# Residual updates in widely spaced pieces beside the feed-forward part, and an S5 input product that opens with two blocks

## The chip, the cores and the metric

The kernel runs on one core of a Trainium2 chip. The metric is the device time of one launch in microseconds (us), as a median of runs. TensorE (PE) does the matrix products, VectorE (DVE), ScalarE (ACT) and GpSimd (POOL) the elementwise work, and SyncE (SP) issues most of the DMAs. TensorE's clock is granted at one of two levels, 1.2 or 2.4 GHz; the profile gives the granted clock of a stretch as a share of the higher one.

## What is computed

One inference step of a two-layer encoder trunk, for 1024 prompt tokens and 32 sample tokens that share all weights (model width 1024, feed-forward width 4096, all in float32):

```
for layer in range(2):
    h = rmsnorm(x, g0);  mix = retention + forgetting attention  (layer 0)   or   S5 state space + GLU  (layer 1)
    x = x + rmsnorm(mix, g1)
    h = rmsnorm(x, g2);  x = x + rmsnorm(cross_attn(h, memory), g3)
    h = rmsnorm(x, g4);  x = x + rmsnorm(square(relu(h @ w_up)) @ w_down, g5)
# S5: u = h @ w_in_c; states x_t = a * x_(t-1) + B u_t; y = C x + D u; then a gate
```

Every `x = x + rmsnorm(...)` is a residual update. The order that matters here: cross-attention and its update in layer 0, feed-forward in layer 0 and its update, the S5 input product of layer 1, the S5 scan, the second layer's memory products, the gate product, and then cross-attention and feed-forward of layer 1.

## The kernel before, in words

Activations lie transposed: 128 rows of the width on the partitions, tokens along the free dimension. The 1056 tokens are cut into three groups of 384, 384 and 288. A float32 product is made of three matmuls of rounded parts (`mm3`, L72: high x high, high x low, low x high), so each weight block is split on arrival into `wh` (ScalarE, L139) and `wl` (VectorE, L140), and each activation tile into `xh` (ScalarE, L201) and `xl` (VectorE, L202). A block of 128 output rows for one group is 8 x 3 = 24 matmuls.

TensorE's instructions run in exactly the order in which the program writes them; the other engines' order is chosen by a scheduler that goes by readiness and by a priority, which is the place in the program minus an offset (300 for update pieces and for evacuations, and 600 for the first weights of the feed-forward part). So the place in the program of a piece of VectorE work only gives its priority, while the place of a matmul is binding.

Small dependent steps are placed among the matmuls by a hand-made order, `po`. It keeps a clock `po.now`, which every matmul advances by its columns / 2400 (in us). `po.later(dt, fn)` puts a step into a queue, due `dt` later; `po.tick()`, called after each three matmuls of a block, runs what is due; `po.until(cond)` runs the next steps at once, due or not, until `cond` holds. `get(out, g, key)` is such a demand for a group's input tiles `X` or its scale row or column `r`.

A residual update (`update`, L247) of one group runs through these steps. `post_scale` sums the squares of the product's output over the width (three matmuls with `ones_c` into a bank `c`, from the accumulator `acc`), and takes the root on GpSimd. `add` broadcasts the result to rows (matmuls into a bank `b`). Then come eight pieces `part(0)` to `part(7)`, one for each 128 rows: load the residual (SP), scale (DVE, L273), add (DVE or POOL, L274), split into `xh` and `xl` for the next product, store the new residual (issued by ACT), and square it and add it to `acc2` (ACT and POOL, L244 and L245). `pre_scale` then sums `acc2` over the width (matmuls into a bank `a`) and takes the root (L220); with `row=True`, `pre_row` broadcasts that to a row `rrow`. The four steps are spaced by `L1, L2, L3, L4 = 3.2, 3.0, 5.1, 2.7` and the pieces by `PU = (1.7, 1.6, 1.4)` us of the order's clock, by group.

`proj_out` makes an output product (here of the cross-attention, `wxo`) and calls `update` for each group when its last block is written. `mlp` then runs the feed-forward part: first group 0 alone (four rounds of eight up blocks and eight down blocks, 64 blocks), then groups 1 and 2 together in eight rounds. It starts as soon as group 0's `X` is there, so the updates of groups 1 and 2 after the cross-attention lie beside the opening of the first group's feed-forward part, and the first group's feed-forward update lies beside the opening of the other two.

The S5 input product is a `gemm` over eight blocks. `gran` says how many blocks are taken at once for group 0, then for group 1, then for group 2. `submit` holds the evacuations back (there is a `hold` until the old pools can be closed) until three blocks wait, and `release` then runs them. An evacuation `evac_u` (L1472) needs the group's `r` row. When a block has all three groups, `s5_block` stores `u` and loads it back as `U` (SP), and places the two steps `states` and `outputs` of the S5 scan for that block: `states` is due at 16.5 after that, and not less than 12 after the block before.

The evacuations' demand is `get(X, g, "r")`, the opening feed-forward's is `x = get(X, 0)`.

Of the kernel before, what the change touches and what calls it, by code (L numbers as in the profile page):

```python
# [63 lines left out]
def _body(tc, A):  # L64
    nc = tc.nc
    MULT, ADD, SUB = ALU.mult, ALU.add, ALU.subtract
    po = _Order(lambda: tc.high_priority(offset=HQ))
# [18 lines left out]
    with es:  # L86
# [29 lines left out]
        HP = 300  # L116
        L1, L2, L3, L4 = 3.2, 3.0, 5.1, 2.7
# [4 lines left out]
        PU = (1.7, 1.6, 1.4)  # L122
# [8 lines left out]
        def wload(src, nk, offset=0):  # L131
            m = src.shape[-1]
            n = nk * m
            st = wp.tile([128, 1040], F32, tag="wst", bufs=2, name="wst")
            dma(st[:, :n], src.rearrange("p k m -> p (k m)"))
            wh = wp.tile([128, 1040], F32R, tag="wh", bufs=4, name="wh")
            wl = wp.tile([128, 1040], F32R, tag="wl", bufs=4, name="wl")
            with tc.high_priority(offset=offset):
                act(wh[:, :n], st[:, :n], AF.Copy)  # L139
                vtt(wl[:, :n], st[:, :n], wh[:, :n].bitcast(F32), op=SUB)  # L140
            return wh, wl
# [21 lines left out]
        def gemm(blocks, load, rhs, evac, gran, done=None, post=None, lead=0, final=(0, 1, 2)):  # L163

            blocks = list(blocks)
            at = 0
            while at < len(blocks):
                n = gran(at) if callable(gran) else gran
                bl = blocks[at : at + n]
                at += n  # L170
                ws = [load(b) for b in bl]
                for g in final if at >= len(blocks) else range(3):
                    i = 0
                    while i < len(bl):
                        w = lead if lead else 1
                        lead = 0
                        pss = [bank()[:, : NG[g]] for _ in range(w)]
                        for k in range(8):
                            s = slice(k * 128, k * 128 + 128)
                            x = rhs(g, k)  # L180
                            for j in range(w):
                                wh, wl = ws[i + j]
                                mm3(pss[j], wh[:, s], wl[:, s], x[0], x[1], k == 0, k == 7)
                            po.tick()
                        for j in range(w):
                            def ev(b=bl[i + j], g=g, ps=pss[j]):
                                with tc.high_priority(offset=HP):
                                    evac(b, g, ps)
                                if post is not None:
                                    post(b, g)  # L190
                            submit(ev)
                        i += w
                    if done is not None and at >= len(blocks):
                        submit(lambda g=g: done(g), False)
# [49 lines left out]
                act(sq[:, :n], src, AF.Square)  # L244
                return gtt(acc[:, :n], acc[:, :n], sq[:, :n], op=ADD)  # L245

        def update(o, g, ys, acc, gpost, xres, xout, last=False, row=False, scale=1.0 / 1024, half=False, r=None):  # L247


            n = NG[g]  # L250
            R = []
            if last:
                for k in range(8):
                    R.append(xtile(g, "r").bitcast(F32))
                    dma(R[k], xres(g, k))

            def post_scale():
                rc = rstd_cols(acc, 3, scale, half, r=None if r is None else r())
                po.later(L2, lambda: add(rc))

            def add(rc):
                ps = bcast_rows(rc, 3)
                X = []
                acc2 = None if last else acc_tile(n, "acc2")

                def part(k):
                    if last:
                        xr, t = R[k], xtile(g, "t").bitcast(F32)
                    else:
                        xr = npl.tile([128, 384], F32, tag="xr", bufs=4, name="xr")[:, :n]  # L270
                        dma(xr, xres(g, k))
                        t = yr[0].tile([128, 384], F32, tag="upd", bufs=4, name="upd")[:, :n]
                    stt(t, ys[k], gall[:, gpost, k : k + 1], ps[:, :n], op0=MULT, op1=MULT)  # L273
                    (gtt if last and k % 2 or r and k < 2 or not r and (g == 2 and k % 4 == 1) else vtt)(t, t, xr, op=ADD)  # L274
                    if last:
                        dma(xout(g, k), t)
                    else:
                        h, l = xtile(g, "h"), xtile(g, "l")
                        split_to(h, l, t, gall[:, gpost + 1, k : k + 1])
                        adma(xout(g, k), t)  # L280
                        X.append((h, l))
                        sumsq(acc2, t, n, k == 0)
                    if k < 7:
                        po.later(PU[g], lambda: part(k + 1))
                        return
                    o["X"] = X
                    if not last:
                        po.later(L3, lambda: pre_scale(acc2))

                part(0)  # L290

            def pre_scale(acc2):
                rc = rstd_cols(acc2, 3, 1.0 / 1024, tag="rc" if row else "rx", ps=ba())
                if row:
                    po.later(L4, lambda: pre_row(rc))
                else:
                    o["r"] = rc

            def pre_row(rc):
                ps = bcast_rows(rc, 3)  # L300
                o["r"] = npl.tile([128, 384], F32, tag="rrow", bufs=3, name="rrow")
                act(o["r"], ps[:, :384], AF.Copy)

            po.later(L1, post_scale)

        def get(out, g, key="X"):
            po.until(lambda: key in out[g])
            return out[g][key]
# [3 lines left out]
        def xscr(p):  # L312
            return lambda g, k: xs_dram[p][g][k][:, :]
# [252 lines left out]
        X = [[], [], []]  # L566
# [40 lines left out]
        with tc.tile_pool(name="m0", bufs=1, reuse_waits="tile") as m0, tc.tile_pool(name="s5p", bufs=1, reuse_waits="tile") as s5p:  # L607
# [17 lines left out]
            for g in range(3):  # L625
                ts = [(t, *TT[t][1:]) for t in range(9) if TT[t][0] == g]
                pss = []
                for half in range(2):
# [3 lines left out]
                    for k in range(8):  # L632
                        wh, wl = wv[half][k // 4]
                        s = slice((k % 4) * 260, (k % 4) * 260 + 260)
                        h, l = X[g][k]
# [84 lines left out]
        for hp in range(2):  # L720
            w2 = [wload(A["wrv"][hp, kh], 4, HP) for kh in range(2)]
            for t in range(9):
                g, i, w = TT[t]
# [379 lines left out]
            yl[0] = left.enter_context(tc.tile_pool(name=f"yl{name}", bufs=1, reuse_waits="tile"))  # L1103
            yr[0] = right.enter_context(tc.tile_pool(name=f"yr{name}", bufs=1, side="right", reuse_waits="tile"))

        def proj_out(nblk, load, rhs, evac_y, gpost, xres, xout, gran=4, lead=0, **kw):

            Y, out, acc = [[None] * 8 for _ in range(3)], [{}, {}, {}], [None] * 3

            def evac(b, g, ps):  # L1110
                if b == nblk - gran:
                    acc[g] = acc_tile(NG[g])
                    for k in range(b * 8 // nblk):
                        sumsq(acc[g], Y[g][k], NG[g], k == 0, "sqa")
                k = b * 8 // nblk
                if Y[g][k] is None:
                    Y[g][k] = ytile(g)
                k = evac_y(Y, b, g, ps)
                if b >= nblk - gran and k is not None:
                    sumsq(acc[g], Y[g][k], NG[g], k == 0, "sqa")  # L1120

            def done(g):
                update(out[g], g, Y[g], acc[g], gpost, xres, xout, **kw)

            gemm(range(nblk), load, rhs, evac, gran, done, lead=lead)
            return out
# [14 lines left out]
        out = proj_out(8, lambda b: wload(A["wout"][b], 8), rhs_m, evac_copy, 1, xin, xscr(0), lead=3)  # L1141
# [264 lines left out]
        def cross_mlp(l, X, p, last, left, right):  # L1406

            gi = l * 6
            O, hids, cas = cross(l, X, left, right)
            left = ExitStack()  # L1410

            def rhs_o(g, k):
                po.until(lambda: O[g][k] is not None)
                return O[g][k]

            def fn():
                po.until(lambda: all(o is not None for og in O for o in og))
                cas.close()
                ypools(left, hids, l)

            hold[0] = fn
            X = proj_out(8, lambda b: wload(A["wxo"][l, b], 8), rhs_o, evac_copy, gi + 3, xscr(p), xscr(p + 1))
            out = [{}, {}, {}]

            def done(g, ys, acc):
                update(out[g], g, ys, acc, gi + 5, xscr(p + 1), xfin if last else xscr(p + 2), last=last, row=True, r=lambda: get(X, g, "r"))

            mlp(l, X, done)
            return out, left, hids
# [45 lines left out]
        def s5_block(f, u):  # L1475
# [54 lines left out]
            def outputs(xg):  # L1530
# [14 lines left out]
            po.later(sd["due"] - po.now, states)  # L1545

        close_after(left, X, (0, 1), s5_start)
        gemm(range(8), lambda b: wload(A["winc"][b], 8, HP if b < 2 else 0), lambda g, k: get(X, g)[k], evac_u, lambda at: 3 if at == 0 else 1,
             post=lambda b, g: s5_block(b, uts.pop(b)) if un[b] == 3 else None, final=(2, 0, 1))
        mem = memory_k(1, 2)  # L1550
        memory_v(1, *mem)
# [176 lines left out]
```

## Time and profile before

| | us |
|---|---|
| median of 3 runs | 3341.2 (3340.61 to 3347.26) |
| the profiled execution | 3348.74 |
| its span, first to last instruction | 3346.9 |
| TensorE busy | 3171.1 (95% of the span) |
| VectorE, ScalarE, GpSimd busy | 1616.1, 1195.6, 922.5 |
| mean granted TensorE clock | 0.975 |

A busy time counts a matmul at either clock, so a slow matmul is busy for longer. What can be won or lost lies in the pauses of TensorE and in the stretches at the lower clock.

### The profile page before, as it was taken

What the parts mean: (1) busy time and instruction counts of PE and PEld (TensorE: products, weight loads), DVE (VectorE), ACT (ScalarE), POOL (GpSimd) and SP (SyncE); (2) the same over time, 40 slices, a digit from 0 to 9 for tenths busy, and PEclk for the clock granted to TensorE, in tenths of its full rate; (3) what the DMA queues carried; (4) which work ended last, traced back from release to release, by engine and by line L of the source; (5) the groups of instructions that cost most, each with busy time, mean ns of one, the idle gap of its engine ahead of it and who ended that gap; (6) DMA issues with size and microseconds to landing.
All of it is one profiled execution on the core that took longest, in us unless ns stands there. A gap on an engine that the chain in (4) does not pass through costs nothing. (4 is left out here: it accounts for less than half of the span.)

```text
span 3346.9 us, 50909 instructions
## 1 busy us (share of the span) xinstructions
PE 3171.1 (95%) x19972; PEld 3066.1 (92%) x19972; DVE 1616.1 (48%) x2820; ACT 1195.6 (36%) x2245; POOL 922.5 (28%) x1182
## 2 busy tenths in 40 slices
PE   7999999998998999999999867999998999999997
PEld 7899986698998999999999867998998999999997
DVE  8843576518436434433334687218427344333333
ACT  5213335525435433422223235225435333322322
POOL 4873431315105211311113343015106111210103
PEclk9999999999999999999999989999999999999998
DMA  5561254114114333322222577114124334322222
GB/s 158 155 203 52 63 143 124 33 53 142 48 56 137 129 126 121 116 67 67 73 76 83 185 225 231 47 51 142 48 67 143 115 122 142 108 76 76 70 68 75
DMA packets 194774, 352.87 MB, mean 105 GB/s; under 512 B 36075, under 2 KB 132556, under 8 KB 194404
## 3 DMA queue, kind: packets, MB, share of 16 engines
q1 hardware_dynamic: 150742, 282.13, 27.4%
q10 hardware_dynamic: 35328, 41.83, 3.7%
q0 software_dynamic: 8464, 25.66, 2.3%
q8 instruction: 157, 2.57, 0.3%
q14 instruction: 83, 0.68, 0.1%
HBM read 287.28 MB, written 66.39 MB: 106 GB/s over the span
## 5 line engine op out<-in xcount | busy, mean ns | idle before, releaser
L72 PE MATMUL mm<-xh,wh 128*128 128x384 f32 (+1 forms) x3168 | 1053.7, 333 | 15.6 <-DVE u L1472 6.1
L72 PE MATMUL mm<-xl,wh 128*128 128x384 f32 (+1 forms) x3168 | 1034.3, 326 | 0.8 <-DVE xl L202 0.8
L72 PE MATMUL mm<-xh,wl 128*128 128x384 f32 (+1 forms) x3168 | 1033.4, 326 | 1.4 <-DVE wl L140 1.4
L72 PE MATMUL mm<-ho,wh 128*128 128x384 f32 (+1 forms) x3456 | 824.0, 324 | 4.2 <-POOL ho L1345 4.2
L140 DVE TENSOR_TENSOR wl<-wst,wh 128x1024 fp32r<-128x1024 f32 (+1 forms) x380 | 476.8, 1255 | 646.8 <-ACT wh L139 645.3
L139 ACT ACTIVATE wh<-wst 128x1024 fp32r<-128x1024 f32 (+1 forms) x380 | 402.4, 1060 | 689.1 <-PE mm L72 638.9
L72 PEld LDWEIGHTS mm<-xh,wh 128*128 128x128 f32 x3168 | 605.4, 191 | 24.3 <-DVE u L1472 6.4
L72 PEld LDWEIGHTS mm<-ho,wh 128*128 128x128 f32 x3456 | 603.0, 188 | 6.7 <-POOL ho L1345 6.7
L72 PEld LDWEIGHTS mm<-xl,wh 128*128 128x128 f32 x3168 | 605.4, 191 | 1.1 <-DVE xl L202 1.1
L72 PEld LDWEIGHTS mm<-xh,wl 128*128 128x128 f32 x3168 | 604.1, 191 | 2.2 <-DVE wl L140 2.1
L72 PE MATMUL mm<-ho,wl 128*128 128x384 f32 (+1 forms) x1728 | 558.1, 323 | 0.0
L1345 POOL TENSOR_TENSOR ho<-u,ho 128x384 fp32r<-128x384 f32 (+1 forms) x192 | 182.5, 951 | 1130.9 <-ACT ho L1344 1113.2
L245 POOL TENSOR_TENSOR acc<-acc,sq 128x384 f32<-128x384 f32 (+2 forms) x259 | 283.2, 1099 | 478.6 <-ACT sq L244 473.0
L72 PEld LDWEIGHTS mm<-ho,wl 128*128 128x128 f32 x1728 | 325.3, 188 | 0.0
L1371 DVE TENSOR_TENSOR y<-y,mm 128x384 f32<-128x384 f32 (+1 forms) x272 | 139.2, 512 | 251.3 <-PE mm L72 251.3
L1342 DVE TENSOR_TENSOR u<-u 128x384 f32<-128x384 f32 (+1 forms) x192 | 104.5, 545 | 192.7 <-ACT u L1341 192.6
L1344 ACT ACTIVATE ho<-u 128x384 fp32r<-128x384 f32 (+1 forms) x192 | 95.5, 498 | 209.8 <-DVE u L1342 209.8
L1341 ACT ACTIVATE u<-mm 128x384 f32<-128x384 f32 (+1 forms) x192 | 86.8, 452 | 172.7 <-PE mm L72 171.6
L202 DVE SCALAR_TENSOR_TENSOR xl<-upd,gall,xh 128x384 fp32r<-128x384 f32 (+1 forms) x120 | 105.1, 877 | 5.5 <-ACT xh L201 5.3
L1206 POOL TENSOR_SCALAR p<-p,mx 128x256 f32<-128x256 f32 (+1 forms) x72 | 36.4, 506 | 241.4 <-DVE mx L1205 142.6
L244 ACT ACTIVATE sq<-y 128x384 f32<-128x384 f32 (+1 forms) x126 | 61.7, 494 | 104.7 <-DVE y L1371 55.2
L72 PE MATMUL mm<-xo,wh 128*128 128x384 f32 (+1 forms) x384 | 93.8, 329 | 0.0
(427 smaller groups left out, 4150.5 us busy)
## 6 DMA issues: line engine op xcount, KB each, us to landing
wst<-in_wup_dram SPq DMA_DIRECT2D x128, 512.0 KB
wst<-in_wdn_dram SPq DMA_DIRECT2D x128, 512.0 KB
xs<-upd ACTq DMA_DIRECT2D x80, 192.0 KB
xr<-xs SPq DMA_DIRECT2D x80, 192.0 KB
wst<-in_wab_dram SPq DMA_DIRECT2D x20, 512.0 KB
wst<-in_wxk_dram SPq DMA_DIRECT2D x16, 512.0 KB
wst<-in_wxv_dram SPq DMA_DIRECT2D x16, 512.0 KB
wst<-in_wxq_dram SPq DMA_DIRECT2D x16, 512.0 KB
```

Of the source, the lines that this page charges most:

```text
L72: return nc.tensor.matmul(out, lhsT, rhs, **kw)
L139: act(wh[:, :n], st[:, :n], AF.Copy)
L140: vtt(wl[:, :n], st[:, :n], wh[:, :n].bitcast(F32), op=SUB)
L202: stt(l, src, gain, h.bitcast(F32), op0=MULT, op1=SUB)
L244: act(sq[:, :n], src, AF.Square)
L245: return gtt(acc[:, :n], acc[:, :n], sq[:, :n], op=ADD)
L1206: nc.gpsimd.tensor_scalar(p, p, mx[:, 3:4], 1.0, op0=MULT, op1=MULT)
L1341: act(t, ps, AF.Relu)
L1342: vtt(t, t, t, op=MULT)
L1344: act(h, t, AF.Copy)
L1345: gtt(lo, t, h.bitcast(F32), op=SUB)
L1371: vtt(Y[o], Y[o], ps, op=ADD)
```

## The change

`update` gets a switch `lax`. With it, the five distances become 10, 8, 14 and 8 us, and 10 us from piece to piece, in place of 3.2, 3.0, 5.1, 2.7 and 1.4 to 1.7. It is set for groups 1 and 2 after the cross-attention, and for group 0 after the feed-forward part, in both layers. Apart from that, the S5 input product takes two blocks at first and not three; all later ones are taken singly, as before.

```
-        def update(o, g, ys, acc, gpost, xres, xout, last=False, row=False, scale=1.0 / 1024, half=False, r=None):
+        def update(o, g, ys, acc, gpost, xres, xout, last=False, row=False, scale=1.0 / 1024, half=False, r=None, lax=False):
...
+            d1, d2, d3, d4, dp = (10.0, 8.0, 14.0, 8.0, 10.0) if lax else (L1, L2, L3, L4, PU[g])
...
-                po.later(L2, lambda: add(rc))
+                po.later(d2, lambda: add(rc))
...
-                        po.later(PU[g], lambda: part(k + 1))
+                        po.later(dp, lambda: part(k + 1))
...
-                        po.later(L3, lambda: pre_scale(acc2))
+                        po.later(d3, lambda: pre_scale(acc2))
...
-                    po.later(L4, lambda: pre_row(rc))
+                    po.later(d4, lambda: pre_row(rc))
...
-            po.later(L1, post_scale)
+            po.later(d1, post_scale)
...
-                update(out[g], g, Y[g], acc[g], gpost, xres, xout, **kw)
+                update(out[g], g, Y[g], acc[g], gpost, xres, xout, lax=g in lax, **kw)
...
-            X = proj_out(8, lambda b: wload(A["wxo"][l, b], 8), rhs_o, evac_copy, gi + 3, xscr(p), xscr(p + 1))
+            X = proj_out(8, lambda b: wload(A["wxo"][l, b], 8), rhs_o, evac_copy, gi + 3, xscr(p), xscr(p + 1), lax=(1, 2))
...
-                update(out[g], g, ys, acc, gi + 5, xscr(p + 1), xfin if last else xscr(p + 2), last=last, row=True, r=lambda: get(X, g, "r"))
+                update(out[g], g, ys, acc, gi + 5, xscr(p + 1), xfin if last else xscr(p + 2), last=last, row=True, r=lambda: get(X, g, "r"), lax=g == 0)
...
-        gemm(range(8), lambda b: wload(A["winc"][b], 8, HP if b < 2 else 0), lambda g, k: get(X, g)[k], evac_u, lambda at: 3 if at == 0 else 1,
+        gemm(range(8), lambda b: wload(A["winc"][b], 8, HP if b < 2 else 0), lambda g, k: get(X, g)[k], evac_u, lambda at: 2 if at == 0 else 1,
```

## Rows read from the trace of the kernel before

**Rows 1.** The page's busy times, and the span and mean granted clock of the core.

```profile
PE 3171.1 (95%) x19972; PEld 3066.1 (92%) x19972; DVE 1616.1 (48%) x2820; ACT 1195.6 (36%) x2245; POOL 922.5 (28%) x1182
...
core 0: 3346.9 us, clock 0.975
```

**Rows 2.** Windows: stretch and length, busy us of each engine (instructions), granted clock, DMA.

```profile
core 0: us, PE busy (x) PEld busy (x) DVE busy (x) ACT busy (x) POOL busy (x), PEclk, DMA share, GB/s
1040.00:1115.00 75.00, 60.18 (x325) 58.76 (x324) 57.09 (x78) 39.38 (x76) 45.86 (x44) 0.84 0.53 169
1360.00:1390.00 30.00, 27.18 (x177) 26.95 (x176) 24.66 (x33) 17.26 (x33) 17.57 (x16) 0.94 0.52 158
1830.00:1890.00 60.00, 51.81 (x313) 49.53 (x312) 40.94 (x69) 21.91 (x43) 27.66 (x33) 0.97 0.69 219
...
1980.00:2100.00 120.00, 82.70 (x599) 80.00 (x598) 90.52 (x114) 53.55 (x90) 37.90 (x42) 0.86 0.72 228
2540.00:2615.00 75.00, 60.73 (x336) 59.30 (x336) 58.87 (x80) 39.58 (x77) 45.16 (x44) 0.86 0.53 161
2700.00:2750.00 50.00, 50.00 (x288) 50.00 (x287) 19.77 (x24) 19.44 (x27) 7.09 (x7) 1.00 0.41 133
```

**Rows 3.** Timeline of PE, both feed-forward openings: start, length, instructions [idle before <-releaser].

```profile
1053.70 1.44 PE L72 MATMUL a<-ones_c,acc 128*128 128x1 f32 x6 [3.45 <-POOL acc L245]
...
1066.18 1.44 PE L72 MATMUL c<-ones_c,acc 128*128 128x1 f32 x6 [3.03 <-POOL acc L245]
...
1083.46 0.83 PE L72 MATMUL a<-ones_c,acc 128*128 128x1 f32 x6 [2.16 <-POOL acc L245]
...
1100.35 1.44 PE L72 MATMUL a<-ones_c,acc 128*128 128x1 f32 x6 [6.07 <-POOL acc L245]
...
2553.55 0.92 PE L72 MATMUL a<-ones_c,acc 128*128 128x1 f32 x6 [2.46 <-POOL acc L245]
```

**Rows 4.** PE's waits, 2540 to 2615 us, then 1360 to 1390: total, times, longest.

```profile
PE a L72 <- POOL acc L245: 10.6, 3, 6.0
PE c L72 <- POOL acc L245: 3.0, 1, 3.0
PE b L72 <- POOL rc L220: 0.6, 1, 0.6
...
PE mm L72 <- ACT u L1341: 2.8, 1, 2.8
```

**Rows 5.** Groups by line: 1040 to 1115 us (POOL, DVE), then 2700 to 2750.

```profile
L245 POOL TENSOR_TENSOR acc<-acc,sq 128x288 f32<-128x288 f32 (+1 forms) x26 | 30.2, 1169 | 8.7 <-ACT sq L244 7.6 <-ACT y L1129 0.6
...
L140 DVE TENSOR_TENSOR wl<-wst,wh 128x1024 fp32r<-128x1024 f32 x12 | 16.4, 1366 | 14.0 <-ACT wh L139 14.0
...
L140 DVE TENSOR_TENSOR wl<-wst,wh 128x1024 fp32r<-128x1024 f32 x13 | 15.9, 1226 | 26.6 <-ACT wh L139 26.6
```

**Rows 6.** PE's waits, 1830 to 1890 us (S5 input product opens).

```profile
PE c L72 <- POOL acc L245: 1.4, 1, 1.4
PE b L72 <- POOL rc L220: 1.0, 1, 1.0
...
PE b L72 <- POOL rc L222: 0.6, 1, 0.6
```

**Rows 7.** Timeline of PE, DVE and POOL around the S5 input product.

```profile
1832.07 0.34 PE L72 MATMUL mm<-xh,wh 128*128 128x384 f32 x1
...
1849.33 1.17 DVE L202 SCALAR_TENSOR_TENSOR xl<-upd,gall,xh 128x384 fp32r<-128x384 f32 x1
...
1854.52 1.06 POOL L220 TENSOR_TENSOR rc<-ms,mhalf 128x3 f32<-128x3 f32 x1 [1.15 <-DVE ms L212]
...
1870.84 0.67 DVE L1472 TENSOR_TENSOR u<-mm,rrow 128x288 f32<-128x288 f32 x1 [4.95 <-PE mm L72]
...
1990.94 0.82 DVE L1472 TENSOR_TENSOR u<-mm,rrow 128x384 f32<-128x384 f32 x1
...
2000.53 0.58 PE L72 MATMUL mm<-xmh,wh 128*128 128x256 f32 x1 [17.60 <-ACT wh L139]
```

More of the change, by code (lines that the diff above doesn't have):

```diff
@@ L1104, in ypools, with proj_out @@
             yr[0] = right.enter_context(tc.tile_pool(name=f"yr{name}", bufs=1, side="right", reuse_waits="tile"))
-        def proj_out(nblk, load, rhs, evac_y, gpost, xres, xout, gran=4, lead=0, **kw):
+        def proj_out(nblk, load, rhs, evac_y, gpost, xres, xout, gran=4, lead=0, lax=(), **kw):
             Y, out, acc = [[None] * 8 for _ in range(3)], [{}, {}, {}], [None] * 3
```

## The prediction

> **What bounds the kernel now.** I read the page first. TensorE is busy 3171.1 of 3346.9 us at a mean granted clock of 0.975 [rows 1]; no other engine passes 48%. The matrix work is the same before and after, so a change can only move two things: the roughly 176 us in which TensorE stands still, and what it loses where the clock was granted at its lower level (1.2 instead of 2.4 GHz). Next I read the windows, to see where both losses sit. In a plain feed-forward stretch TensorE is busy 50.00 of 50 us at clock 1.00, with VectorE at 40% and GpSimd at 14% [rows 2]: nothing to gain there. At the two places where the cross-attention residual update runs beside the opening of the feed-forward part (1040 to 1115 us, and 2540 to 2615 us in layer 1) TensorE is busy only 60.18 and 60.73 of 75 us at clock 0.84 and 0.86, while VectorE is busy 57 to 59 us [rows 2]. The clock falls only around these pauses: it is 1.00 where TensorE does not stop.
>
> Then I asked the timeline what ended each pause. In layer 0 there are four, and the reader should see that all four are the same instruction pattern: a tiny matmul with `ones_c`, the one in `rstd_cols` that sums a group's squares, waits for `acc` from L245 on GpSimd [rows 3]: 3.45, 3.03, 2.16 and 6.07 us, together 14.71. No pause is for a weight or a hidden tile. By the order in which the program issues them they are: `pre_scale` of group 0, `post_scale` of group 2, `pre_scale` of group 1, `pre_scale` of group 2. Layer 1 repeats it: 10.6 us for `a`, 3.0 for `c`, 0.6 for a broadcast, 14.2 in all [rows 4]. TensorE runs in the written order, so one tiny matmul that is due 3 to 5 us after its predecessor stops all matrix work when VectorE and GpSimd are behind.
>
> **The change, part by part.**
>
> *Part 1, `lax=(1, 2)` on the cross-attention output.* No instruction is added or removed; tiny matmuls and the pieces of groups 1 and 2 move later in the written order. Group 2's `post_scale` goes from 3.2 to 10 us after the group's last block: it waited 3.03 us, and gets 6.8 us more, so this wait is gone. Each `pre_scale` stood 7 x 1.6 + 5.1 = 16.3 us (group 1) or 7 x 1.4 + 5.1 = 14.9 us (group 2) behind its broadcast; it now stands 7 x 10 + 14 = 84 us behind it. Even if VectorE and GpSimd do the pieces in the same burst as now, these two matmuls arrive some 68 us later than they do today, against waits of 2.16 and 6.07 us. Gone in layer 0: 3.03 + 2.16 + 6.07 = 11.3 us. In layer 1, of `a` 10.6 the part of group 0 (2.46 [rows 3]) stays: 8.1 + 3.0 + 0.6 = 11.7 us. The end fits: group 2 is done about 10 + 8 + 70 + 14 = 102 us after its last block, and nobody reads it until the first group's feed-forward part is over, 64 blocks of 24 matmuls later, 64 x 4.17 = 267 us (288 matmuls take 50 us [rows 2]).
>
> Clock: the two stretches lose 60.18 x 0.16 = 9.6 and 60.73 x 0.14 = 8.5 us of matrix work to the low level. I give it back in proportion to the pauses that go: 9.6 x 11.3 / 14.7 = 7.4 and 8.5 x 11.7 / 14.2 = 7.0. Bounds: nothing (the remaining pause is enough to drop the clock as often) to all 18.1.
>
> Group 0 is not spaced out, so its `pre_scale` (3.45 and 2.46 us) keeps its place. But the sixteen pieces that shared VectorE and GpSimd with it now come later; I take half, 3.0, with 1.5 of clock. Bounds 0 and 5.9 + 3.8.
>
> *Part 2, `lax` on the first group's feed-forward update.* Its pieces now lie beside groups 1 and 2. In layer 0 this update costs 2.8 us, a matmul waiting for ScalarE's `u` [rows 4], plus 27.18 x 0.06 = 1.6 us of clock [rows 2]. The first four or five pieces can still be taken early (they are issued with a head start of 300 places in the program order, 300 x 50 / 288 = 52 us of matmuls [rows 2]), so I take 3.0; bounds 0 and 4.4. In layer 1 I count nothing: no wait row there bears on it.
>
> *What spacing costs.* Forty pieces (16 + 16 + 8) move beside plain feed-forward work. There VectorE is idle 60% of the time [rows 2], which hides them; without that cover each could delay a hidden tile or a weight. From below zero: the 16 pieces now beside the opening delay no weight and no tile. From above: eight bunched pieces in layer 0 cost 2.8 + 1.6 = 4.4, 0.55 each, so 40 x 0.55 = 22. I take 2.5, near the low end, because spaced pieces resemble the opening with less load.
>
> *Part 3, the S5 product opens with two blocks.* Removed from the front: block 2 for groups 0 and 1, 2 x 4.17 = 8.3 us of cover; moved behind group 2. Its DMAs and weight split move with it; SP has no queue there that this lengthens. What is late next: today group 1's product begins after three blocks. Now its first block would end about 1832.07 + 3 x 4.17 + 3.8 = 1848.4 (3.8: waits of 1.4 and 0.6 [rows 6] and two tiny matmul groups of 0.9), while the last split of group 1's input ends at 1849.33 + 1.17 = 1850.5 [rows 7]: 2 us. The deferred evacuations are released at the third waiting block, which is now group 1's first; that one needs group 1's broadcast row, so the program pulls `pre_row` forward to directly behind it. Its `rc` comes off GpSimd at 1855.6 [rows 7], and TensorE waited 1.0 us for it even with a block in between [rows 6]: now, by estimate from these rows, 3 to 4 us. Group 2 repeats it with its own row, about 2.5. Sum 8 to 9 us of new waits against 8.3 us of cover removed: block 0's last `u` (1870.84 [rows 7]) stays where it is, and the S5 chain starts no earlier. TensorE is 8 us behind with its own blocks. That is mostly absorbed: at the end of this product TensorE waits 17.6 us for a weight [rows 7]; the last `u` is written only at 1990.94 by a VectorE busy 90.52 of 120 us [rows 2, 7], and behind it on SP stand the loads for that weight. I take a loss of 4. Bounds: a gain of 8 (the chain does start a block earlier) and a loss of 9 + 5 of clock.
>
> *Sum.* 11.3 + 7.4 + 11.7 + 7.0 + 3.0 + 1.5 + 3.0 - 2.5 - 4.0 = 38.4 us. The profiled execution took 3348.74 us, span 3346.9 plus 1.8 around it: 3310.3. That run is 7.5 above the median of the three shown; against the median it is 3341.2 - 38.4 = 3302.8.
>
> **Rivals.**
>
> *A, the S5 product pays its upper bound*, 14 instead of 4 us: 3313. For it: waits of 1.4, 1.0 and 0.6 us for GpSimd already sit in its first 60 us [rows 6], with VectorE busy 40.94 of 60 [rows 2]. Against it: the 17.6 us pause behind it.
>
> *B, the spaced pieces hurt the feed-forward part: slower.* In place of one burst, 40 times a GpSimd add and two-input VectorE operations come between the weight splits. The split took 1366 ns on average beside the burst, and 1226 in the clean stretch [rows 5]. If each piece's add (1169 ns [rows 5]) held up one split for its whole length, and the split were what TensorE waits for, that is 47 us of pauses; at 0.65 us of clock loss per us of pause (9.6 / 14.7) it is 77 us, so 3341 - 41 + 77 = 3377. It decides from 0.62 us of pause per piece: 40 x 0.62 x 1.65 = 41, all that the rest brings. Against it: 0.14 us per split is what the burst costs, on an engine that waits 26.6 of 50 us for ScalarE [rows 5].
> The Trainium skill, "SBUF — State Buffer", section "Who interferes with whom", says that a VectorE instruction with two SBUF inputs and a GpSimd instruction that reads SBUF exclude each other, the later one blocking fully. By that rule alone every overlap costs up to a whole add, which is rival B at 3377; the stretched splits agree that they collide, their size does not bear out the price.
>
> *C, the order moves but the work does not.* If VectorE still takes all pieces in one burst, only the written order of the tiny matmuls changed. The waits go all the same; group 0's relief and Part 2 fall away: 38.4 - 7.5 = 30.9, 3310.
>
> *D, given back.* The S5 chain is bound by VectorE and queues, and its order may fall out anew; a loss there of 35 us, twice its largest pause now, would leave 3338, no difference.
>
> **How the numbers follow.** Chances: forecast 0.52, A 0.15, C 0.15, all faster; D 0.09, same; B 0.09, slower. 0.2% is 6.7 us, about what this measurement can tell from no change. I predict 3303. Low end: S5 gains 8 instead of losing 4 (12) and group 0 is relieved in full (5): 3286. High end: A, C and 15 of the 22 us for the pieces: 3341 - 38 + 10 + 8 + 15 = 3336, short of D and B.
>
> **What would show it.** Right: in the profile after, no `c` or `a` matmul waits for L245 beside the first group's feed-forward part except group 0's; TensorE is busy over 70 of the same 75 us and the granted clock there is over 0.95; the 2.8 us for ScalarE's `u` is gone. In the S5 product, new waits for `rc` and `xl` in the first 40 us, with block 0's last `u` within 3 us of its present distance from the product's start. Wrong: matmuls that wait for weights or hidden tiles all along the feed-forward part (B), or a longer stretch between the product's start and the first gate matmul by over 15 us (D).

## The result, and the profile after

| | before | after |
|---|---|---|
| median, us | 3341.29 (3340.61 to 3347.26) | 3308.86 (3308.30 to 3310.08) |
| ratio, 95% interval | | 0.990 (0.9882 to 0.9917) |
| span of the profiled execution | 3346.9 | 3307.2 |
| mean granted TensorE clock | 0.975 | 0.979 |

The change saves 32.4 us by the medians and 39.7 by the two profiled spans. The forecast was 3303, range 3286 to 3336, so the time came out as forecast. Its parts did not. To see that, lay both traces beside each other at five points that the program passes in both: the first `c` matmul after the cross-attention of each layer; in each layer, in the fourth round of the first group's feed-forward part, the matmul by which the first down block takes in the last hidden tile; and group 1's `c` ahead of the S5 input product. An opening, in this table, runs from a layer's `c` to that matmul.

| stretch | before, us | after, us | gained | forecast |
|---|---|---|---|---|
| start to layer 0's `c` | 1023.60 | 1020.27 | 3.3 | 0 |
| opening of the feed-forward part, layer 0 | 298.26 | 288.74 | 9.5 | } 39.4 |
| opening of the feed-forward part, layer 1 | 296.49 | 289.32 | 7.2 | } with spacing |
| end of layer 0's feed-forward part, its update | 499.73 | 498.16 | 1.6 | 3.0 |
| S5 product to layer 1's `c` | 702.37 | 683.72 | 18.6 | -4.0 |
| the rest | 526.45 | 526.99 | -0.5 | 0 |

(39.4 is the forecast's waits and clock of both openings, 37.4, plus group 0's 4.5, less 2.5 for the spacing.) The gains add up to 39.7. The first 3.3 us are not the change's: up to there the program is the same in both kernels, and over the fourteen traces of this document that stretch takes between 1017.9 and 1025.6 us. The openings brought 16.7 us, less than half of what was forecast, and the stretch of the S5 product, forecast as a small loss, brought more than both of them.

The page and the core's row after, the columns as in [rows 1]:

```profile
PE 3164.6 (96%) x19972; PEld 3059.5 (93%) x19972; DVE 1619.8 (49%) x2820; ACT 1195.5 (36%) x2245; POOL 925.3 (28%) x1182
...
core 0: 3307.2 us, clock 0.979
```

The windows after, at the same points of the program as in [rows 2] (both openings, then the end of the S5 input product, shifted by 14 us):

```profile
1036.70:1111.70 75.00, 66.24 (x371) 64.96 (x370) 55.81 (x73) 40.13 (x76) 40.34 (x37) 0.89 0.54 167
2507.00:2582.00 75.00, 65.48 (x368) 64.21 (x367) 55.31 (x73) 39.54 (x75) 38.32 (x37) 0.89 0.51 160
...
1966.00:2086.00 120.00, 101.77 (x707) 98.83 (x706) 84.87 (x109) 55.48 (x91) 32.27 (x36) 0.91 0.67 210
```

The openings rose from 60 to 66 of 75 us, not to over 70, and the clock to 0.89, not to over 0.95. The S5 window rose from 82.70 to 101.77 of 120.

The timeline of TensorE in both openings after (start, length, instructions, and in brackets the idle time before it and what ended it):

```profile
1049.85 1.44 PE L72 MATMUL a<-ones_c,acc 128*128 128x1 f32 x6 [3.85 <-POOL acc L245]
...
1100.95 0.69 PE L72 MATMUL mm<-ho,wh 128*128 128x384 f32 x1 [4.18 <-ACT ho L1345]
1102.10 0.69 PE L72 MATMUL mm<-ho,wh 128*128 128x384 f32 x1 [0.47 <-POOL ho L1346]
...
1166.32 0.72 PE L72 MATMUL a<-ones_c,acc 128*128 128x1 f32 x6
1180.28 0.72 PE L72 MATMUL a<-ones_c,acc 128*128 128x1 f32 x6
...
2521.26 1.44 PE L72 MATMUL a<-ones_c,acc 128*128 128x1 f32 x6 [4.60 <-POOL acc L245]
...
2572.24 0.69 PE L72 MATMUL mm<-ho,wh 128*128 128x384 f32 x1 [4.17 <-ACT ho L1345]
```

Set this beside [rows 3]. The waits of groups 1 and 2 are gone: their `a` matmuls run at 1166 and 1180 us and wait for nothing. Group 0's wait is still there, and longer (3.85 for 3.45, and 4.60 for 2.46). A new one stands where the first down block needs the last hidden tile (`ho`): 4.2 us in each layer, where the kernel before had 0.5.

Why that tile is late can be read from ScalarE and VectorE. ScalarE writes the last block's `u`, VectorE squares it, and `ho` is made from the square. The timeline in layer 0, first of the kernel after, then of the one before:

```profile
1096.16 0.47 ACT L1342 ACTIVATE u<-mm 128x384 f32<-128x384 f32 x1
1096.34 0.60 DVE L274 SCALAR_TENSOR_TENSOR upd<-y,gall,b 128x384 f32<-128x384 f32 x1
1096.86 0.60 DVE L202 SCALAR_TENSOR_TENSOR xl<-upd,gall,xh 128x384 fp32r<-128x384 f32 x1
1097.39 1.34 DVE L275 TENSOR_TENSOR upd<-upd,xr 128x384 f32<-128x384 f32 x1
1098.66 1.21 DVE L140 TENSOR_TENSOR wl<-wst,wh 128x1024 fp32r<-128x1024 f32 x1
1099.79 0.55 DVE L1343 TENSOR_TENSOR u<-u 128x384 f32<-128x384 f32 x1
...
1114.61 0.47 ACT L1341 ACTIVATE u<-mm 128x384 f32<-128x384 f32 x1
1114.74 1.23 DVE L140 TENSOR_TENSOR wl<-wst,wh 128x1024 fp32r<-128x1024 f32 x1 [2.55 <-ACT wh L139]
1115.88 0.55 DVE L1342 TENSOR_TENSOR u<-u 128x384 f32<-128x384 f32 x1
```

After the change, VectorE does three operations of update pieces and a weight split first, and takes up the last `u` 3.2 us after ScalarE wrote it; before, 0.8 us. ScalarE itself was 3.6 us behind the last up matmul; before, 0.8.

The S5 input product after, the timeline of TensorE beside [rows 6, 7], and below it VectorE's row of block 0's last `u`:

```profile
1835.86 0.44 PE L72 MATMUL mm<-xl,wh 128*128 128x384 f32 x1 [1.59 <-DVE xl L202]
1838.60 1.65 PE L72 MATMUL b<-ident,rc 128*128 128x128 f32 x6 [1.35 <-POOL rc L220]
...
1850.67 0.40 PE L72 MATMUL mm<-xl,wh 128*128 128x288 f32 x1 [1.18 <-DVE xl L202]
1853.23 1.21 PE L72 MATMUL b<-ident,rc 128*128 128x128 f32 x6 [1.47 <-POOL rc L220]
1874.61 0.69 PE L72 MATMUL a<-U,Gm 128*128 128x132 f32 x4 [0.36 <-issue]
...
1973.77 1.22 PE L72 MATMUL a<-U,Gm 128*128 128x132 f32 x4 [4.27 <-DMA yf<-yd]
1983.78 0.58 PE L72 MATMUL mm<-xmh,wh 128*128 128x256 f32 x1 [4.30 <-DVE u L1473]
```

```profile
1855.00 0.68 DVE L1473 TENSOR_TENSOR u<-mm,rrow 128x288 f32<-128x288 f32 x1 [1.41 <-ACT rrow L303]
```

The forecast new waits for `xl` and `rc` are there, and block 0's last `u` comes 47.8 us after group 1's `c` (1807.17), before 49.3. But the pause of 17.60 us [rows 7] is gone, with 4.30 in its place.

### The profile page after: what moved, and what is told of

It is laid out like the page before. It is cut to its first block, busy times and chain, and to the rows that moved or that the text cites. A ratio compares the mean times of both kernels' runs of the same rounds, so it can differ in the third digit from the quotient of the medians.

```text
span 3307.2 us, 50897 instructions
## 1 busy us (share of the span) xinstructions
PE 3164.6 (96%) x19972; PEld 3059.5 (93%) x19972; DVE 1619.8 (49%) x2820; ACT 1195.5 (36%) x2245; POOL 925.3 (28%) x1182
## 4 chain that ended last, share of the span: by engine, by line
PE 79%; DVE 9%; issue 3%; DMA 3%; POOL 2%; ACT 2%; SPq 0%; ACTq 0%; DVEq 0%; POOLq 0%
PE mm L72 70%; PE a L72 5%; PE b L72 2%; PE c L72 1%; DVE wl L140 1%; DVE xl L202 1%; POOL acc L245 1%; DVE upd L275 1%; DVE upd L274 1%; PE b L76 1%; ACT wh L139 0%; DMA yf<-yd 0%; POOL rc L220 0%; DVE p L1514 0%; POOL ho L1346 0%
```

## The experiments

Each ratio is to the kernel before, with its 95% interval.

### The three parts one by one

`s5_two`: the kernel before with the two-block opening alone.

```
-... evac_u, lambda at: 3 if at == 0 else 1,
+... evac_u, lambda at: 2 if at == 0 else 1,
```

> The kernel before with only the two-block opening of the S5 input product. Theory 1 (the two-block opening itself is what shortens the S5 stretch, which is 18 us shorter in the changed kernel between the `c` matmul of group 1 and the gate product): 3341 - 18 = 3323, and the 17.6 us wait for the first memory weights falls below 6. Theory 2 (as predicted: new waits eat the block of cover, and the 18 us come from the order falling out anew after the updates moved): 3341 + 4 = 3345, the 17.6 us wait stays above 12.

`xo_only`: the spacing after the cross-attention alone (`lax=(1, 2)` in `proj_out`).

> The kernel before with only the switch on groups 1 and 2 after the cross-attention. Theory 1: each opening of the feed-forward part is worth 7 to 10 us, so 3341 - 17 = 3324, and the S5 stretch keeps its 17.6 us wait. Theory 2 (the S5 stretch is shortened by the shifted order alone): 3341 - 17 - 18 = 3306. The prediction's own sum for this part (20 us in each layer) would give 3301 with no help from the S5 stretch.

`ff_only`: the spacing of the first group's feed-forward update alone (`lax=g == 0` in `done`).

> The kernel before with only the switch on the first group's feed-forward update. Both theories: 2 to 3 us in layer 0 around its opening of groups 1 and 2, so 3338 to 3339; the 2.8 us wait for ScalarE's u is gone or under 1. If the S5 stretch moves too by more than 5 us, its order depends on more than its own code.

| | median, us | ratio | gain |
|---|---|---|---|
| s5_two | 3326.95 | 0.9961 (0.9946 to 0.9976) | 15.8 |
| xo_only | 3327.09 | 0.9957 (0.9940 to 0.9973) | 15.6 |
| ff_only | 3340.21 | 0.9995 (0.9985 to 1.0005) | 2.5, not resolved |

The gains (against 3342.73, the median of before in this series) sum to 33.9 by the medians and to 29 by the ratios; the whole change has 32.4. So there is no sign that the parts depend on each other. The two-block opening gains by itself.

### Does the spacing of the pieces matter, or only the place of the tiny matmuls?

`burst`: the changed kernel with the old distances between pieces, and `pre_scale` kept where the change put it.

```
-... d1, d2, d3, d4, dp = (10.0, 8.0, 14.0, 8.0, 10.0) if lax else ...
+... d1, d2, d3, d4, dp = (10.0, 8.0, 84.0 - 7 * PU[g], 8.0, PU[g]) if lax else ...
```

> The changed kernel with the pieces of the switched updates as close together in the written order as before (1.4 to 1.7 us), and the matmuls of the steps around them left where the change puts them. Theory 1 (the pieces run in a burst on VectorE and GpSimd anyway, because a place in the program is only a priority there; what the change moves is the tiny matmuls): 3309 within 4 us, and the 16 pieces beside the opening take about 53 us on VectorE as in the changed kernel. Theory 3 (the spacing of the pieces is what helps): at least 10 us slower, 3319 or more.

Measured: 3332.8 us, 0.9973 (0.9963 to 0.9982), 23.9 slower than the changed kernel. My own theory, that only the place of the matmuls counts, is wrong. Its opening of layer 0 takes 295.29 us, nearly the 298.26 of before; the opening of layer 1 and the end of layer 0's feed-forward part are 7.1 us longer each than in the changed kernel. The timeline of TensorE in `burst`, at the first step from up to down blocks and in the feed-forward update:

```profile
1096.64 1.01 PE L72 MATMUL mm<-ho,wh 128*128 128x384 f32 x2 [5.37 <-ACT u L1342]
...
1104.85 0.44 PE L72 MATMUL mm<-ho,wh 128*128 128x384 f32 x1 [2.07 <-ACT ho L1345]
...
1107.87 0.69 PE L72 MATMUL mm<-ho,wh 128*128 128x384 f32 x1 [1.33 <-ACT ho L1345]
...
1382.23 1.01 PE L72 MATMUL mm<-ho,wh 128*128 128x384 f32 x2 [5.81 <-ACT u L1342]
```

The pieces begin at about the same time in both kernels, but do not run at the same pace: from the first piece to the start of the last split VectorE takes 42 us here (1063.7 to 1105.6) and 52 in the changed kernel (1065.0 to 1117.3), where it starts the third piece 13 us after the second and here 4. Bunched, they come ahead of the hidden tiles: these are late, and TensorE waits for them and no longer for the `acc` of groups 1 and 2. (Group 0's wait of 3.85 us is in both.) Why a written distance of 10 us turns into this pace is not shown. A piece written farther back has a lower priority and could yield, but the next run speaks against a simple form of that.

`low_prio`: the changed kernel, its spaced pieces and broadcasts issued without the head start of 300 places.

```
-                        po.later(dp, lambda: part(k + 1))
+                        po.later(dp, lambda: part(k + 1), lax)
...
-        with self.first():
+        with ExitStack() if lo else self.first():
```

> The changed kernel, with the pieces and broadcasts of the spaced updates issued without their head start of 300 places; written distances stay. Theory 1 (the burst of the pieces runs early only because of the head start, and delays the split of the hidden tiles for the first down blocks): the pieces spread out beyond 1130 us, the 4.18 and 4.17 us waits for ho at the first step from up to down blocks vanish with their part of the clock loss, 3293 to 3302. Theory 2 (the pieces fill gaps anyway and the wait for ho comes from the length of the chain from the last up matmul to the first down matmul): the wait stays within 1 us, 3306 to 3312. Slower than 3315 would mean that pieces now come too late for a later matmul, which would show as waits of a matmuls for acc or of the broadcast for rc.

Measured: 3307.7 us, 0.9903 (0.9890 to 0.9916), no difference from the changed kernel. Theory 2 holds: VectorE's pieces did not spread (the last `xl` starts at 1120.09, there 1117.28, with TensorE itself 5 us later in this run), and the wait for `ho` is 3.22 and 0.71 us where it was 4.18 and 0.47. The head start is not what runs them early, and a priority lower by 300 places is not enough to spread them.

### Group 0's step, which the change left where it was

`g0_late`: the changed kernel, with group 0's `pre_scale` after the cross-attention 60 us after its last piece.

```
-... if lax else (L1, L2, L3, L4, PU[g])
+... if lax else (L1, L2, 60.0 if gpost in (3, 9) else L3, L4, PU[g])
```

> The changed kernel with one more step moved: group 0's pre_scale after the cross-attention comes 60 us after its last piece in place of 5.1, in both layers. In the changed kernel its matmul still waits 3.85 us (layer 0) and 4.60 us (layer 1) for acc. Theory 1 (a wait that a written distance too short causes goes when the distance grows, and takes its share of the clock loss along): both waits vanish, TensorE is busy over 69 of the 75 us in both openings, 8.5 us of waits plus 4 to 8 of clock, 3292 to 3302 against 3308.9. Theory 2 (the opening is bound by VectorE and GpSimd, so a wait removed comes back at the next matmul that needs them, as the 4.18 us wait for ho did): the wait at the first step from up to down blocks grows by about as much, 3305 to 3311.

Measured: 3291.04 us (3290.04 to 3293.76), 0.9854 (0.9841 to 0.9866), another 17.8 us below the changed kernel. The windows of `g0_late` at the same points of the program, then the timeline of TensorE in layer 0's opening:

```profile
1034.32:1109.32 75.00, 71.09 (x424) 70.28 (x423) 49.44 (x63) 39.63 (x70) 29.83 (x26) 0.98 0.56 176
2496.05:2571.05 75.00, 70.37 (x412) 69.42 (x412) 49.99 (x64) 39.40 (x70) 28.76 (x26) 0.95 0.55 169
```

```profile
1088.53 0.44 PE L72 MATMUL mm<-ho,wh 128*128 128x384 f32 x1 [2.87 <-ACT ho L1345]
1089.79 0.45 PE L72 MATMUL mm<-ho,wh 128*128 128x384 f32 x1 [0.81 <-POOL ho L1346]
```

Both waits for `acc` are gone, the wait for `ho` did not grow but fell to 2.87, and the clock is back at 0.98 and 0.95. Theory 1 holds. The openings shrink to 279.27 and 281.29 us: 9.5 and 8.0 below the changed kernel, for waits of 3.85 and 4.60. (In layer 1 one wait of 1.14 us for ScalarE's `y` is new.)

`g0_only`: the same step moved in the kernel before, and nothing else.

```
-                        po.later(L3, lambda: pre_scale(acc2))
+                        po.later(60.0 if gpost in (3, 9) and g == 0 else L3, lambda: pre_scale(acc2))
```

> The kernel before with group 0's pre_scale after the cross-attention 60 us after its last piece, and nothing else: no spaced pieces, no two-block opening. Theory 1 (each early matmul costs its own wait and its share of the clock, whatever the others do): the waits of 3.45 and 2.46 us go, those of groups 1 and 2 stay, about 3.5 to 9 us gained, 3332 to 3338. Theory 2 (the openings of both updates have one cause, a burst on VectorE and GpSimd, and a wait that is taken away comes back at the next matmul): the waits of groups 1 and 2 grow by as much, 3338 to 3343.

Measured: 3341.91 us, 1.0002 (0.9994 to 1.0011): no gain. The timeline of TensorE in `g0_only`, layer 0, beside [rows 3]:

```profile
1061.74 1.44 PE L72 MATMUL c<-ones_c,acc 128*128 128x1 f32 x6 [5.39 <-POOL acc L245]
1078.38 0.83 PE L72 MATMUL a<-ones_c,acc 128*128 128x1 f32 x6 [2.16 <-POOL acc L245]
1095.86 1.44 PE L72 MATMUL a<-ones_c,acc 128*128 128x1 f32 x6 [5.05 <-POOL acc L245]
```

Of the 3.45 us taken away, 2.36 came back at once at the next matmul that needs GpSimd (3.03 became 5.39). So the same edit is worth 18 us in the changed kernel and nothing that can be measured in the kernel before: here theory 2 is nearer. As long as another tiny matmul stands soon behind, TensorE mostly waits there instead. The trace does not go all the way with theory 2: the four waits still sum to 12.6 us where they were 14.7, and the opening of layer 0 is 4.5 us shorter, while the other traces of kernels with the old opening lie within 1 us of each other (297.4 to 298.4). The next two stretches are 1.2 and 0.9 us longer; where the rest of these 4.5 us went stays open.

### What the S5 opening does

`s5_one`: the changed kernel, opening with one block (`lambda at: 1`).

> The changed kernel with the S5 input product opening with one block, not two. Theory 1 (what the opening with fewer blocks gives is that block 0 is finished for all groups earlier, so the scan chain starts earlier and the later weight loads come earlier): block 0's last u and the first scan step come some 4 to 8 us nearer to the product's start, 3300 to 3306. Theory 2 (two blocks already bring all of it, since the wait for memory weights is gone; one block only takes cover away at the opening): waits for the splits of groups 1 and 2 and for their scales grow from about 6 to 12 to 18 us, and the scan starts no earlier, 3310 to 3320.

Measured: 3322.08 us, 0.9946 (0.9934 to 0.9958), 13.2 slower than with two. It fits theory 2 in sign, 2 us beyond its range. The timeline of TensorE shows the larger price of this opening: its waits up to block 0's last `u` sum to 15.2 us, against 8.0 with two blocks. Two of them, for GpSimd's `rc`:

```profile
1828.47 1.65 PE L72 MATMUL b<-ident,rc 128*128 128x128 f32 x6 [5.77 <-POOL rc L222]
...
1853.28 1.65 PE L72 MATMUL b<-ident,rc 128*128 128x128 f32 x6 [2.10 <-POOL rc L220]
```

`k_act`: the kernel before, with the memory keys' weights loaded from ScalarE's queue. In the kernel before, the third of these loads was issued at 1993.55 us on SP, behind a store of `u` at 1991.79, and its `wh` ended the pause of 17.60 us; in the changed kernel that load is issued at about 1909.

```
...
-                ws = [wload(A["wxk"][l, b], 8) for b in bl]
+                ws = [wload(A["wxk"][l, b], 8, q=adma if l else None) for b in bl]
```

> The kernel before (three blocks at the opening, no spacing) with one edit: the weights of the second layer's memory keys are loaded from ScalarE's DMA queue in place of SP's. Theory 1 (the 17.6 us pause at the end of the S5 input product is the third of these loads standing on SP behind the store of u, which VectorE writes late; opening with two blocks brings these loads ahead of that store): the load comes at least 10 us earlier, the pause falls below 6 us, 3322 to 3334 against 3341.3. Theory 2 (the pause is the whole chain of the product being late, VectorE and the scan included; the load is only the last in line): another wait of 10 us or more, for u, yf or Tm, takes its place, 3337 to 3343.

Measured: 3344.65 us, 1.0011 (1.0001 to 1.0021). The third load is now issued at 1911.94 and the pause for `wh` is gone, but the time is not. The timeline of TensorE, and the row of ScalarE that explains the first wait:

```profile
1962.92 1.25 PE L72 MATMUL a<-U,Gm 128*128 128x132 f32 x4 [8.29 <-ACT yt L1538]
1988.33 0.58 PE L72 MATMUL mm<-xmh,wh 128*128 128x256 f32 x1 [5.67 <-DVE u L1472]
...
2023.21 1.22 PE L72 MATMUL a<-U,Gm 128*128 128x132 f32 x4 [5.11 <-DMA U<-ud]
...
2057.14 0.58 PE L72 MATMUL mm<-wh,xmh 128*128 128x256 f32 x1 [7.38 <-DVE mo L363]
```

```profile
1961.76 0.33 ACTq L135 DMA_DIRECT2D wst<-in_wxk_dram  x1
1962.20 0.39 ACT L1538 ACTIVATE yt<-b 128x264 f32<-128x264 f32 x1 [13.21 <-DVE xml L202]
```

Theory 2 fits, 1.7 us beyond its range and with a reservation: 8.29 us of the new waits are the edit's own, because ScalarE stood 13.21 us ahead of the issue of its fifth load and could not evacuate `yt`. (The row names VectorE's `xml`; the load was issued at 1961.76, right behind a split that ended at 1961.73; a split reads one of the kernel's two load buffers, so that this one became free then is likely, not shown.) The other three still hold 18 us. The late load was the last in line, not the cause.

`s1_early` and `s1_late` move the due time of only the first scan step of the S5 chain: earlier in the kernel before, later in the changed one. The later steps keep their rule, and so can follow it. In `s1_late` the 9.5 below is 23.5.

```
-            sd["due"] = max(po.now + S1, sd.get("due", 0.0) + 12.0)
+            sd["due"] = max(po.now + (S1 if f else 9.5), sd.get("due", 0.0) + 12.0)
```

> The kernel before (three blocks at the opening, no spacing) with one edit: the first scan step is due 9.5 us after block 0 is handed to it, not 16.5; the later steps keep their rule of 16.5 us and at least 12 after the one before. In the kernel before the first scan step comes 73.1 us after group 1's c, with its U loaded some 8 us earlier, and in all three kernels that open with two blocks at about 67.5. Theory 1 (opening with two blocks gains because the scan chain starts earlier): the first step moves to about 66 to 68 us after group 1's c, the end of the memory products from 262.5 us after it to 246 to 255, 3324 to 3334 against 3341. Theory 2 (the chain's start is not what counts; the order of the blocks behind the opening, and with it of u and of VectorE's work, is): the stretch keeps its length within 4 us, 3337 to 3343.

> The counterpart: the changed kernel with the first scan step due 23.5 us after block 0 is handed to it, not 16.5. Theory 1: the first step moves from 67.4 to about 74 us after group 1's c, as in the kernel before, and most of the 16 us that the stretch gained is lost, 3318 to 3326 against 3308.9. Theory 2: the scan only starts later and catches up, 3305 to 3312.

Measured: `s1_early` 3326.86 us, 0.9956 (0.9942 to 0.9970), 14.5 gained with three blocks at the opening; `s1_late` 3326.79, 0.9958 (0.9946 to 0.9971), 17.9 lost with two. Theory 1 holds from both sides (`s1_late` 0.8 us beyond its range). The timeline of TensorE in `s1_early`, the first scan step, then in `s1_late` that step and the old pause:

```profile
1880.57 0.69 PE L72 MATMUL a<-U,Gm 128*128 128x132 f32 x4 [0.44 <-DMA U<-ud]
```

```profile
1882.87 0.61 PE L72 MATMUL a<-U,Gm 128*128 128x132 f32 x4
...
1982.93 0.58 PE L72 MATMUL mm<-xmh,wh 128*128 128x256 f32 x1 [13.41 <-ACT wh L139]
```

In `s1_early` the step waits 0.44 us for `U`: it stands right behind its data. In `s1_late` the pause for the memory weights is back, with two blocks at the opening. In us after group 1's `c` (the end is the start of the last memory matmul):

| | first scan step | end of the memory products |
|---|---|---|
| before | 73.1 | 262.5 |
| s1_late | 72.6 | 261.0 |
| k_act | 71.4 | 265.2 |
| g0_only | 71.3 | 262.6 |
| xo_only, ff_only | 70.7 | 260.9, 260.2 |
| s5_one | 68.4 | 258.6 |
| low_prio | 67.9 | 247.5 |
| s5_two | 67.7 | 246.3 |
| after, g0_late | 67.4 | 246.2, 247.3 |
| burst | 67.3 | 246.3 |
| combo | 65.9 | 246.5 |
| s1_early | 63.5 | 243.8 |

It is a step, not a slope: from 70.7 on the stretch ends at 260 or later, up to 67.9 between 243 and 248. `s5_one` (68.4, and 258.6) lies just between; whether its start or its other order of blocks makes it slow was not tried.

`combo`: `g0_late`, with three blocks at the opening and the early first scan step in place of two blocks.

> The best kernel so far (the changed one with group 0's pre_scale 60 us later, 3291.0) with the two-block opening of the S5 product replaced by three blocks and a first scan step due at 9.5 us. Theory 1 (two blocks act only through the start of the scan chain, and the parts of the change are independent): the start alone does the same, and the kernel does not pay the opening's waits for xl and rc; the stretch from group 1's c to the end of the memory products was 243.8 us with the early step and 246.2 with two blocks, so 3285 to 3292. Theory 2 (two blocks do something else as well): 3294 or more.

Measured: 3295.29 us (3290.36 to 3296.58), 0.9860 (0.9839 to 0.9881). The interval holds that of `g0_late`, and both theories' times lie within it: a tie that decides nothing. That `g0_late` at 3291.0 beats both kernels stands: its interval, 0.9841 to 0.9866, lies below that of the change, 0.9882 to 0.9917.

## Why the prediction was right, point by point

**The waits of groups 1 and 2: right.** 11.3 and 11.7 us were to go, and went [rows 3, 4].

**Their sum over the opening: mis-sized, 16.7 us measured against 39.4.** Two steps failed. First, "No pause is for a weight or a hidden tile" was true of the kernel before and was carried over to the kernel after. The work on ScalarE, VectorE and GpSimd did not get less; it now stands in the way at the next place where TensorE needs these engines, the first step from up to down blocks, whose waits grew by 4.4 us per layer (0.5 to 4.9). `g0_only` shows the same in small (2.36 of 3.45 us came back). Second, the clock was given back in proportion to the pauses (7.4 and 7.0 us). Measured, at low clock are lost 66.24 x 0.11 = 7.3 and 65.48 x 0.11 = 7.2 us, before 9.6 and 8.5: 2.3 and 1.3 came back. Two pauses of 4 us left in each opening kept most of the loss, near the lower bound named there. In layer 0 the terms now nearly add up: 11.3 less 4.4 for `ho` less 0.4 for group 0 plus 2.3 of clock is 8.8, measured 9.5.

**Group 0's relief (3.0 and 1.5): wrong.** Its wait grew. Its cause was its own distance of 5.1 us: `g0_late` moves it and gets 17.5 us from both openings.

**Part 2 (3.0): 1.6 by the traces**, and the same in `ff_only` (498.15 us for this stretch); by the medians alone not resolved. The 2.8 us for `u` became 1.21 for `wl` and 0.93 for `u`.

**Spacing costs 2.5: not seen as a cost, but not tested as it was meant.** `burst` shows the opposite sign: spaced pieces are worth 24 us, because the hidden tiles then come less late. But the pieces did not come to lie among plain feed-forward work: the sixteen still ran within 52 us beside the opening, the eight of the feed-forward update within 21. So rival B's time is refuted, while its price, for pieces that really lie among the weight splits, was not measured; after the openings the first group's feed-forward part waits 0.5 us at each step from up to down blocks, as before. The rule of the Trainium skill beside it ("SBUF — State Buffer", "Who interferes with whom"), that a VectorE instruction with two SBUF inputs contends with a GpSimd instruction that reads SBUF, was isolated by no run here.

**The S5 opening (-4.0, bounds +8 and -14): wrong in sign and outside its bounds, +18.6 by the traces, 15.8 as a part alone.** Right were the new waits in kind (`xl` and `rc`: 5.6 us, forecast 8 to 9), and that block 0's last `u` would stay where it is (47.8 for 49.3). The second held because the clock made up for the smaller waits: up to that `u` all waits sum to 8.0 us for 4.8, and the granted clock is 0.92 for 1.00, which costs another 3. The step that failed is the next one, "and the S5 chain starts no earlier". The chain's first step is not tied to `u`; it is due 16.5 us of the written order after block 0 is handed over, and the hand-over stands earlier in that order by block 2's products for groups 0 and 1, 8.3 us. In the kernel before, `U` was on its way by 1883.76 (the last of eight issues of its load on SP), and the step ran at 1894.74. It had slack, and the change used 5.7 us of it (73.1 to 67.4). The windows over these two stretches, before and then after, show why it was not 8.3: TensorE stands for 8.2 and 8.4 us, so the new waits and the old ones weigh the same, but loses 1.3 and 4.7 us to the clock. That leaves 4.7 of the 8.3, near the 5.7 measured:

```profile
1821.59:1894.74 73.15, 64.97 (x410) 62.68 (x409) 48.38 (x83) 25.35 (x48) 34.43 (x39) 0.98 0.65 200
```

```profile
1807.17:1874.61 67.44, 59.08 (x356) 56.96 (x355) 47.52 (x80) 25.18 (x48) 34.25 (x39) 0.92 0.64 200
```

About 2 of the 5.7 us lie between two profiles of the same S5 code: `xo_only`, `ff_only` and `g0_only` start the step at 70.7 to 71.3. Shown is that moving the chain's first step is enough, both ways (`s1_early`, `s1_late`); why 3 us of it, between 67.9 and 70.7, bring 13 at the end was not taken apart; the order on VectorE and on SP behind that step is a likely way, not a shown one. The 17.6 us pause, which the forecast used as cushion, is one form of that delay: it comes with a late chain (17.60, `xo_only` 15.77, `s1_late` 13.41) and not with an early one, and taking it away by itself gave nothing.

**Rivals.** A and D asked what S5 would cost and are refuted by its sign; D's mechanism, that the chain's order falls out anew, is what happened. C (the order moves, the work does not) is half right: the pieces do stay a burst, of 52 us, but its pace matters. The time 3308.9 lies near C's 3310 for other reasons. That the total came out was luck: two errors, 23 us too much in the openings and 23 too little in S5, cancelled.

## What to carry to other kernels

Where TensorE runs in a written order, a wait that one removes is worth its length or more only if the next instruction that needs the same engines stands far enough behind; move all the early ones of a burst together (18 us for the last one, nothing measurable for it alone). Before one prices a moved block by the data it makes, look up what the next step's place is tied to: a step written well behind its data can gain from an edit that only moves its mark, and can be moved directly (14.5 us here). When a total comes out right, still check it stretch by stretch between points that both kernels pass.

## What the runs showed of the hardware

How the granted clock answers to one pause surprised me. The windows of the changed kernel, 25 us each, right behind the 3.85 us wait at 1046 to 1049.85 us and after it, and last the first window of `burst`, which stands behind a wait of 3.85 us too:

```profile
1050.00:1075.00 25.00, 25.00 (x133) 25.00 (x134) 10.56 (x16) 9.58 (x17) 8.67 (x12) 0.83 0.38 122
1075.00:1100.00 25.00, 21.50 (x124) 20.86 (x122) 23.24 (x31) 14.45 (x27) 13.30 (x11) 0.99 0.63 193
...
1050.00:1075.00 25.00, 25.00 (x140) 25.00 (x141) 14.50 (x22) 10.55 (x19) 10.40 (x13) 0.89 0.49 145
```

TensorE is busy for all of the first 25 us and has the lower clock (1.2 GHz) for a part of them, at a mean of 0.83: 4.2 us of matrix work lost behind a pause of 3.85. In the second it stands for 3.5 us and has 0.99. So the loss falls behind the pause, and a stretch with 100% busy time is not one at full speed. Nor does one pause have one price: behind the same wait `burst` has 0.89, 2.8 us lost. In `g0_late`, where 2.87 and 0.81 us of waiting are left at one place, the opening of layer 0 runs at 0.98.
